# Seven products for both halves of a down-projection's columns, in an encoder trunk on one core

## The chip, the core and the metric

The kernel runs on one core of a Trainium2 chip. The metric is the device time of one execution in microseconds (us). The core's engines are TensorE (PE in the profile; its weight loads are PEld), VectorE (DVE), ScalarE (ACT), GpSimd (POOL) and SyncE (SP, which issues most transfers). Each works through its own instructions in the program's order and meets the others at semaphores.

## The reference

Two layers over 256 positions of 2048 channels, all float32. Each layer is a mixer (pooling and attention in layer 0, a bidirectional mLSTM in layer 1) and then a gated MLP. The change concerns the MLP alone:

```
def conv_ffn(x, w_up, conv_w, conv_b, w_down):     # D_MODEL 2048, D_FF 5632
    u = x @ w_up                                   # 2 * D_FF columns
    up = jnp.pad(u, ((0, 0), (1, 1), (0, 0)))
    u = c[0] * up[:, :-2] + c[1] * up[:, 1:-1] + c[2] * up[:, 2:] + conv_b
    gate, val = jnp.split(u, 2, axis=-1)
    return (jax.nn.silu(gate) * val) @ w_down      # 5632 x 2048

x = x + conv_ffn(rms_norm(x, norm_ffn[layer]), w_up[layer], ..., w_down[layer])
```

## The kernel before

**Arithmetic.** Every float32 operand of a matmul is split into a high part (rounded to TensorE's fp32r) and a low part, the remainder. A product is three matmuls: high by high, high by low, low by high. Weights are split on the fly: ScalarE casts a raw tile to its high part (L120), VectorE subtracts to get the low part (L121).

**The weight stream.** All weights pass through one list of tiles of 128 x 1024 (512 KB), in the order in which TensorE needs them (class Stream, L79 to L142). Raw tiles (w) have six buffers, split tiles (hl) four. Loads go out on SP up to five tiles ahead, splits are placed up to two tiles ahead of the use. Two kinds of entry are special. A `Sum` tile is loaded on SP from one array, and a second array is then added into it by an accumulating transfer that GpSimd issues (L105, L106); Sum tiles have two buffers and are prepared up to ten entries ahead. A `Chain` tile's raw weights get the Sum tile before it added to their first half (L116), and that half is then added to their second half (L117), both on VectorE, before the split.

**One gated MLP** (ffn_layer, L906). The 5632 hidden channels are 44 tiles of 128, in chunks of 4, 8, 8, 8, 8, 8 (FCH, L33). For each hidden tile an *up* (L924) multiplies 2048 channels into gate and value: four weight tiles, 64 matmuls. Its result is gathered (L400, L401), scaled (L928), convolved (L933 to L937), gated (L941, L942) and split into g (L943, L944). The 128 gated channels of 256 positions are two quarters of 128 x 128.

**Down-projection.** The 2048 columns are four blocks of 512. For chunks 0 to 4, blocks 0 and 1 go the ordinary way (down, L1040): for each block the chunk's hidden tiles are accumulated in PSUM and added to x (residual, L407). Blocks 2 and 3 use a 2x2 scheme of seven products instead of eight (Strassen's, in Winograd's form): two hidden tiles by two position tiles on one side, two hidden tiles by two blocks on the other. The sums of g quarters are formed and split by combine (L948); the sums of weight blocks come from Sum and Chain tiles and from a tile prepared on the host. A *unit* A (L968) does four of the products of one pair of hidden tiles (two weight tiles, 12 matmuls), a unit B three (one and a half weight tiles, 9 matmuls). Over a chunk each product accumulates in one PSUM bank; at the end of the chunk's A or B units the banks are added to seven kept sums acc (L991 to L995). After chunk 4 the seven sums are combined into x by eleven additions (total, L999). The last chunk does all four blocks the ordinary way, each in full before the next.

**What sets the order.** _ffn_plan (L1129) writes out the order of ups, units and downs: while chunk c's ups run, the units and the two downs of chunk c - 1 lie between them, one unit per up. The instructions of TensorE stay in this written order. The order on the other engines is set by a scheduler that simulates the kernel while building it. Small tasks (class Weave, L145) are started by estimated time.

Of the kernel before, what the change touches and what calls it, by code (L numbers as in the profile page):

```python
# [31 lines left out]
FT = DFF // P  # L32
FCH = [4, 8, 8, 8, 8, 8]  # L33
CH = 8
NEG = -1.0e30
NGATE = 96 + 8
WARM = 5
# [153 lines left out]
def trunk(ctx: ExitStack, tc: tile.TileContext, gx, xT, xn, call, catt, cml, weights, out):  # L191
# [714 lines left out]
    def ffn_layer(layer, norm, nxt):  # L906
        with ExitStack() as es:
# [7 lines left out]
            combos, pss = {}, {}  # L915

            def cw(tl, j):
                c = C_CONV + layer * 88 * 4 + tl * 4 + j
# [5 lines left out]
            def up(c, f, gt, i):  # L924
                ps = stat_group(xx, list(range(KT)), f"up{layer}_{f}")
                wv.until(lambda: norm.R is not None)
                u = gather(tp, ps, f"up{layer}_{f}")
                v.tensor_mul(u, u, bc(norm.R, 2))  # L928
                y = tp.tile([P, 2, S], F32, tag="y", name=f"y{layer}_{f}")
                z = t1p.tile([P, 2, 2, S], F32, tag="z", name=f"z{layer}_{f}")  # L930
                for j in range(2):
                    tl = f + j * FT
                    a.activation(z[:, 0, j, :], u[:, j, :], AF.Copy, scale=cw(tl, 0))  # L933
                    a.activation(z[:, 1, j, :], u[:, j, :], AF.Copy, scale=cw(tl, 2))
                    a.activation(y[:, j, :], u[:, j, :], AF.Identity, scale=cw(tl, 1), bias=cw(tl, 3))  # L935
# [4 lines left out]
                s_ = pair[-1][:, i % 2 * 2 : i % 2 * 2 + 2].rearrange("p a b -> p (a b)")  # L940
# [3 lines left out]
                v.tensor_sub(gt[:, i, 1, :], s_, gt[:, i, 0, :].bitcast(F32))  # L944
                if i % 2 and c < len(FCH) - 1:
                    combine(c, i // 2, pair[-1])

            def combine(c, j, g4):  # L948

                sf = t1p.tile([P, 4, P], F32, tag="sf", name=f"sf{layer}_{c}_{j}")  # L950
                v.tensor_sub(sf[:, 0:2], g4[:, 0::3], g4[:, 1:2].to_broadcast([P, 2, P]))
# [13 lines left out]
                mm(ps, xl, wh, False, last)  # L965
                wv.tick(0.68)

            def unit(kind, c, j):  # L968

                n = FCH[c] // 2  # L970
                order = (4, 6, 5, 3) if kind == "A" else (0, 1, 2)
                if j == 0:
                    for e in order:
                        pss[e] = psp.tile([P, 512], F32, tag="ps", name=f"pp{layer}_{c}_{e}")
                gt = gts[c]
                s3, s1 = combos[c, j]

                def part(k, t):
                    return [gt[:, 2 * j + k, i, t * P : t * P + P] for i in range(2)]

                if kind == "A":
                    xs = [[s3[:, i, m] for i in range(2)] for m in (1, 0, 2)] + [part(1, 1)]
                else:
                    xs = [part(0, 0), part(1, 0), [s1[:, i] for i in range(2)]]
                for m, e in enumerate(order):
                    if m % 2 == 0:
                        hl = st.next()
                    wh, wl = (hl[:, i, m % 2 * 512 : m % 2 * 512 + 512] for i in range(2))
                    product(pss[e], xs[m], wh, wl, j == 0, j == n - 1)
                if j == n - 1:  # L990
                    for e in order:  # L991
                        if c == 0:
                            a.copy(acc[:, e], pss[e])
                        else:
                            v.tensor_add(acc[:, e], acc[:, e], pss[e])  # L995
                    if kind == "B" and c == len(FCH) - 2:
                        wv.add(total(), 12.0)

            def total():  # L999

                p1, p2, p3, q4, p5, q6, p7 = (acc[:, e] for e in range(7))
                x00, x01, x10, x11 = (x[:, t, c : c + 512] for t in range(2) for c in (1024, 1536))
                steps = [(q6, v.tensor_sub, p1), (x10, v.tensor_sub, q6), (x10, v.tensor_add, p7),
                         (x10, v.tensor_add, q4), (x00, v.tensor_add, p1), (x00, v.tensor_add, p2),
                         (q6, v.tensor_sub, p5), (x01, v.tensor_add, q6), (x01, v.tensor_sub, p3),
                         (x11, v.tensor_add, q6), (x11, v.tensor_sub, p7)]
# [3 lines left out]
                pss["total"] = True  # L1010

            def down_end(gt, b, kts):

# [26 lines left out]
            def down(c, b):  # L1040
                gt, last = gts[c], c == len(FCH) - 1
                kts = list(range(FCH[c]))
                if last and nxt is None and b == NB - 1:
                    down_end(gt, b, kts)
                    return
                ps = mmp.tile([P, 2, 512], F32, tag="mm", name=f"dn{layer}_{c}_{b}")
                mov_part(ps, lambda k: gt[:, k], kts, True, True)
                if last and b >= 2:
                    wv.until(lambda: "total" in pss)
                residual(ps, b)  # L1050
                if last and nxt is None:
                    nc.sync.dma_start(out[:, :, b * 512 : b * 512 + 512], x[:, :, b * 512 : b * 512 + 512])
                elif last:
                    nxt.add(b)

            wv.add(norm.finish(), 4.0)
            f, gts, pair = 0, [], []
            for kind, c, i in _ffn_plan():
                if kind == "up":
                    if i == 0:  # L1060
                        gts.append(actp.tile([P, 8, 2, S], F32R, tag=f"B{c % 2}", name=f"g{layer}_{c}"))
# [1 line left out]
                    f += 1  # L1063
                elif kind == "down":
                    down(c, i)
                else:
                    unit(kind, c, i)

    norms = [Norm(0), None]
    norms[1] = Norm(1)  # L1070
# [55 lines left out]
    return np.ascontiguousarray(t.transpose(4, 0, 2, 1, 3, 5)).reshape(FT * (KT // 4), P, CH * P)  # L1126


def _ffn_plan():  # L1129

    seq = []
    for c, n in enumerate(FCH):
        pairs = FCH[c - 1] // 2 if c else 0
        for i in range(n):
            seq.append(("up", c, i))
            if i < 2 * pairs:
                seq.append(("AB"[i // pairs], c - 1, i % pairs))  # L1140
            for b in range(2):
                if pairs and i == (b + 1) * pairs // 2 - 1:
                    seq.append(("down", c - 1, b))
    return seq + [("down", len(FCH) - 1, b) for b in range(NB)]


def _down_chunks(w):
# [2 lines left out]
    out, k0 = [], 0  # L1150
    for c, n in enumerate(FCH):
        rows = w[k0 * P : (k0 + n) * P]
        out += [_mov(rows[:, b * 512 : b * 512 + 512]) for b in range(2 if c < len(FCH) - 1 else NB)]
        k0 += n
    n = sum(FCH[:-1]) // 2
    b = w[: 2 * n * P, 1024:].reshape(n, 2, P, 2, 512)
    b11, b12, b21, b22 = (b[:, k, :, c] for k in range(2) for c in range(2))

    def two(a, b):
        return np.concatenate([a, b], axis=2)  # L1160

    return np.concatenate(out), two(b12, b12), two(b11, b22), two(b22, b21), two(b11, b21), b22


def _ffn_weights(up, parts):

    down, s0, s1, r, ba, bb = parts
    out, u, d = [], 0, 0
    starts = []
    for c, n in enumerate(FCH):  # L1170
        starts.append(d)
        d += n // 2 * (2 if c < len(FCH) - 1 else NB)
    for kind, c, i in _ffn_plan():
        q = sum(FCH[:c]) // 2 + i
        if kind == "up":
            out += up[u : u + 4]
            u += 4
        elif kind == "down":
            n = FCH[c] // 2
            out += down[starts[c] + i * n : starts[c] + i * n + n]  # L1180
        elif kind == "A":
            out += [Sum(s0[q], s1[q]), Chain(r[q])]
        else:
            out += [ba[q], bb[q]]
    return out


# [98 lines left out]
```

## Time and profile before

| | before |
|---|---|
| median of 3 runs | 2185.68 us (2185.67 to 2186.78) |
| the profiled execution | 2185.79 us |
| its span | 2184.0 us |
| gated MLP of layer 0, first to last up | about 256 to 932 us of the span |
| gated MLP of layer 1, first to last up | about 1458 to 2135 us |
| bytes moved | 462.95 MB, 212 GB/s on the average |

The span is the time from the first to the last instruction that the profiler shows. Busy times are shares of the span; a matmul's end is modelled, so a TensorE that is busy all the time isn't necessarily at its peak. In a row of instructions, "out<-in" names the tiles written and read, "x12" is a count, and a bracket or a last column names what ended the idle time before. "Landing" is the time from a transfer's issue to its completion. A chunk's part of the MLP in which eight ups run with the previous chunk's units and downs is called a full stage below; there are four in a layer (chunks 2 to 5), and the one of chunk 1 carries half as much down work.

### The profile page before, as it was taken

What the parts mean: (1) busy time and instruction counts of PE and PEld (TensorE: products, weight loads), DVE (VectorE), ACT (ScalarE), POOL (GpSimd) and SP (SyncE); (2) the same over time, 40 slices, a digit from 0 to 9 for tenths busy, and PEclk for the clock granted to TensorE, in tenths of its full rate; (3) what the DMA queues carried; (4) which work ended last, traced back from release to release, by engine and by line L of the source; (5) the groups of instructions that cost most, each with busy time, mean ns of one, the idle gap of its engine ahead of it and who ended that gap; (6) DMA issues with size and microseconds to landing.
All of it is one profiled execution on the core that took longest, in us unless ns stands there. A gap on an engine that the chain in (4) does not pass through costs nothing.

```text
span 2184.0 us, 31216 instructions
## 1 busy us (share of the span) xinstructions
PE 2176.3 (100%) x11508; PEld 1862.4 (85%) x11508; DVE 1668.1 (76%) x2358; ACT 1373.8 (63%) x2174; POOL 59.3 (3%) x76
## 2 busy tenths in 40 slices
PE   9999999999999999999999999999999999999999
PEld 7888888888888888889888888888888888888887
DVE  7686687887878788786767676668788787878876
ACT  7665577766667576666555554557776676757663
POOL 0010000000000000000000000000000000000000
PEclk9999999999999999999999999999999999999999
DMA  9556567676777766656565555756768677776664
GB/s 322 182 169 203 175 205 228 210 243 208 249 231 245 223 226 219 217 187 205 161 201 180 181 179 176 224 177 202 229 207 245 207 246 235 246 228 221 219 217 153
DMA packets 133595, 462.95 MB, mean 212 GB/s; under 512 B 14810, under 2 KB 17154, under 8 KB 133442
## 3 DMA queue, kind: packets, MB, share of 16 engines
q1 hardware_dynamic: 125024, 438.08, 60.0%
q0 software_dynamic: 5344, 19.14, 5.2%
q10 hardware_dynamic: 3074, 3.75, 0.7%
q8 instruction: 90, 1.47, 0.3%
q14 instruction: 63, 0.52, 0.1%
HBM read 458.76 MB, written 2.14 MB: 211 GB/s over the span
## 4 chain that ended last, share of the span: by engine, by line
PE 99%; DVE 0%; ACT 0%; issue 0%
PE up L237 45%; PE dn L237 12%; PE op L237 8%; PE pp L237 8%; PE mv L237 4%; PE mq L237 4%; PE mk L237 4%; PE mo L237 4%; PE qproj L237 3%; PE kproj L237 1%; PE pool L237 1%; PE vproj L237 1%; PE qk L237 1%; PE av L237 1%; PE end L237 0%; PE xt L288 0%
## 5 line engine op out<-in xcount | busy, mean ns | idle before, releaser
L121 DVE TENSOR_TENSOR hl<-w,hl 128x1024 fp32r<-128x1024 f32 (+2 forms) x808 | 951.7, 1192 | 256.9 <-ACT hl L120 254.5
L120 ACT CAST hl<-w 128x1024 fp32r<-128x1024 f32 (+2 forms) x807 | 817.1, 1028 | 460.9 <-PE up L237 143.7
L237 PE MATMUL up<-xx,hl 128*128 128x512 f32 (+1 forms) x5632 | 993.6, 337 | 0.0
L237 PEld LDWEIGHTS up<-xx,hl 128*128 128x128 f32 x5632 | 867.0, 188 | 130.4
L237 PE MATMUL dn<-hl,g 128*128 128x512 f32 x1200 | 278.5, 390 | 2.5 <-DVE g L944 2.3
L237 PEld LDWEIGHTS dn<-hl,g 128*128 128x128 f32 x1200 | 224.5, 188 | 50.8 <-DVE g L944 3.2
L400 ACT COPY tb_up<-up 128x512 f32<-128x512 f32 x88 | 51.7, 587 | 135.3 <-PE up L237 135.3
L237 PE MATMUL pp<-hl,s 128*128 128x512 f32 x432 | 111.2, 393 | 0.0
L401 DVE TENSOR_TENSOR tb_up<-up,tb_up 128x512 f32<-128x512 f32 x88 | 60.7, 690 | 57.0 <-ACT tb_up L400 57.0
L935 ACT ACTIVATE y<-tb_up,cst 128x256 f32<-128x256 f32 x176 | 103.8, 590 | 0.0
L936 DVE TENSOR_TENSOR y<-y,z 128x510 f32<-128x510 f32 x88 | 60.6, 688 | 52.9 <-ACT y L935 52.4
L933 ACT ACTIVATE z<-tb_up,cst 128x256 f32<-128x256 f32 x176 | 88.5, 503 | 12.2 <-DVE tb_up L928 12.0
L237 PE MATMUL mk<-xx,hl 128*128 128x512 f32 (+1 forms) x512 | 92.2, 337 | 0.0
L237 PE MATMUL mq<-xx,hl 128*128 128x512 f32 (+1 forms) x512 | 92.1, 337 | 0.0
L237 PE MATMUL mv<-hl,xx 128*128 128x512 f32 (+2 forms) x480 | 91.7, 350 | 0.0
L237 PE MATMUL op<-hl,cat 128*128 128x512 f32 x384 | 91.6, 393 | 0.0
L237 PEld LDWEIGHTS pp<-hl,s 128*128 128x128 f32 x432 | 78.5, 188 | 15.1
L237 PE MATMUL mo<-hl,xx 128*128 128x512 f32 x384 | 90.4, 391 | 0.0
L237 PE MATMUL op<-hl,mcat 128*128 128x512 f32 x384 | 89.5, 392 | 0.0
L237 PEld LDWEIGHTS mq<-xx,hl 128*128 128x128 f32 x512 | 79.2, 188 | 11.6
L237 PEld LDWEIGHTS mk<-xx,hl 128*128 128x128 f32 x512 | 79.0, 188 | 11.4
L237 PEld LDWEIGHTS mv<-hl,xx 128*128 128x128 f32 x480 | 78.3, 189 | 11.2
(229 smaller groups left out, 1985.4 us busy)
## 6 DMA issues: line engine op xcount, KB each, us to landing
w<-in_up SPq DMA_DIRECT2D x352, 512.0 KB, 4.3
w<-in_dn SPq DMA_DIRECT2D x176, 512.0 KB, 4.5
w<-in_m_in SPq DMA_DIRECT2D x124, 512.0 KB, 4.1
w<-in_a_in SPq DMA_DIRECT2D x46, 512.0 KB, 4.4
sum<-in_dn SPq DMA_DIRECT2D x36, 512.0 KB, 4.6
sum<-in_dn POOLq DMA_DIRECT2D x36, 512.0 KB, 7.4
w<-in_a_out SPq DMA_DIRECT2D x32, 512.0 KB, 3.5
w<-in_m_out SPq DMA_DIRECT2D x32, 512.0 KB, 4.0
```

Of the source, the lines that this page charges most:

```text
L120: (self.nc.vector.tensor_copy if i + c == 0 else self.nc.scalar.copy)(hl[:, 0, c : c + n], w[:, c : c + n])
L121: self.nc.vector.tensor_sub(hl[:, 1, c : c + n], w[:, c : c + n], hl[:, 0, c : c + n].bitcast(F32))
L237: pe.matmul(out_, lhsT, rhs, start=start, stop=stop, skip_group_check=True)
L400: a.copy(tb, ps[:, :, 1, :])
L401: v.tensor_add(tb, ps[:, :, 0, :], tb)
L933: a.activation(z[:, 0, j, :], u[:, j, :], AF.Copy, scale=cw(tl, 0))
L935: a.activation(y[:, j, :], u[:, j, :], AF.Identity, scale=cw(tl, 1), bias=cw(tl, 3))
L936: v.tensor_add(y[:, :, 1:S], y[:, :, 1:S], z[:, 0, :, 0 : S - 1])
```

## The change

Blocks 0 and 1 of chunks 0 to 4 now go through the seven products too, so the columns have two halves (h = 0, 1) with units of their own. Where two halves of eight units stand against eight ups, two units follow each up: AA, AA, BB, BB for half 0, then the same for half 1. Sum and Chain tiles double. Instead of seven kept sums there are three per half: the products that enter only one quarter of the result are added to x at once at the end of a chunk's units, the others to the kept sums; total has six additions per half. The combines are placed in the plan ("mix"), each not ahead of the last A unit that reads the same buffers. In the last chunk, blocks 0 and 1 are done together: hidden tiles 0 to 5 for block 0 and for block 1, then tiles 6 and 7 for each.

```diff
+BOTH = (0,1,2,3,4)
...
-            acc = kp.tile([P, 7, 512], F32, tag="acc", name=f"acc{layer}")
+            acc = kp.tile([P, 2, 3, 512], F32, tag="acc", name=f"acc{layer}")
...
-                    pair.append(tp.tile([P, 4, P], F32, tag="silu", name=f"s{layer}_{f}"))
+                    quads[c, i // 2] = tp.tile([P, 4, P], F32, tag="silu", bufs=3, name=f"s{layer}_{f}")
...
-            def unit(kind, c, j):
+            def unit(kind, c, h, j):
...
-                if j == n - 1:
-                    for e in order:
-                        if c == 0:
-                            a.copy(acc[:, e], pss[e])
+                if j < n - 1:
+                    return
+                x00, x01, x10, x11 = parts_of_x(h)
+                if kind == "A":
+                    for to, e in zip(range(3), order):
+                        to = acc[:, h, to]
+                        if h in seen:
+                            v.tensor_add(to, to, pss[e])
                         else:
-                            v.tensor_add(acc[:, e], acc[:, e], pss[e])
-                    if kind == "B" and c == len(FCH) - 2:
-                        wv.add(total(), 12.0)
+                            a.copy(to, pss[e])
+                    seen.add(h)
+                    v.tensor_add(x10, x10, pss[3])
+                else:
+                    v.tensor_add(x00, x00, pss[0])
+                    v.tensor_sub(acc[:, h, 2], acc[:, h, 2], pss[0])
+                    v.tensor_add(x00, x00, pss[1])
+                    v.tensor_sub(x01, x01, pss[2])
+                    if c == len(FCH) - 2:
+                        wv.add(total(h), 12.0 if h else 2.0)
...
+            def down_two(c):
+
+                gt, n = gts[c], FCH[c]
+                pss2 = [mmp.tile([P, 2, 512], F32, tag="mm", name=f"dn{layer}_{c}_{b}") for b in range(2)]
+                for kts in (range(n - 2), range(n - 2, n)):
+                    for ps in pss2:
+                        mov_part(ps, lambda k: gt[:, k], list(kts), kts[0] == 0, kts[-1] == n - 1)
+                wv.until(lambda: 0 not in seen or ("total", 0) in pss)
+                for b, ps in enumerate(pss2):
+                    residual(ps, b)
...
+def _halves(c):
+
+    return () if c == len(FCH) - 1 else (0, 1) if c in BOTH else (1,)
...
         pairs = FCH[c - 1] // 2 if c else 0
+        units = [(kind, c - 1, h, j) for h in (_halves(c - 1) if c else ()) for kind in "AB" for j in range(pairs)]
+        per = max(1, len(units) // n)
+
+        busy = {u[3]: k // per for k, u in enumerate(units) if u[0] == "A"}
         for i in range(n):
             seq.append(("up", c, i))
-            if i < 2 * pairs:
-                seq.append(("AB"[i // pairs], c - 1, i % pairs))
-            for b in range(2):
-                if pairs and i == (b + 1) * pairs // 2 - 1:
-                    seq.append(("down", c - 1, b))
-    return seq + [("down", len(FCH) - 1, b) for b in range(NB)]
+            seq += units[i * per : i * per + per]
+            if len(_halves(c - 1)) == 1:
+                for b in range(2):
+                    if pairs and i == (b + 1) * pairs // 2 - 1:
+                        seq.append(("down", c - 1, b))
+            if c < len(FCH) - 1:
+                seq += [("mix", c, j) for j in range(n // 2) if i == max(2 * j + 1, busy.get(j, 0))]
+    return seq + [("two", len(FCH) - 1, 0)] + [("down", len(FCH) - 1, b) for b in range(2, NB)]
```

More of the change, by code (lines that the diff above doesn't have):

```diff
@@ L1065, in ffn_layer @@
                     down(c, i)
+                elif kind == "two":
+                    down_two(c)
+                elif kind == "mix":
+                    combine(c, i)
                 else:
-                    unit(kind, c, i)
+                    unit(kind, c, i, *j)
     norms = [Norm(0), None]
@@ L1152, in _down_chunks @@
         rows = w[k0 * P : (k0 + n) * P]
-        out += [_mov(rows[:, b * 512 : b * 512 + 512]) for b in range(2 if c < len(FCH) - 1 else NB)]
+        blocks = [_mov(rows[:, b * 512 : b * 512 + 512]) for b in range(NB) if b // 2 not in _halves(c)]
+        if c == len(FCH) - 1:
+            b0, b1 = blocks[:2]
+            blocks[:2] = [b0[:-1], b1[:-1], b0[-1:], b1[-1:]]
+        out += blocks
         k0 += n
     n = sum(FCH[:-1]) // 2
-    b = w[: 2 * n * P, 1024:].reshape(n, 2, P, 2, 512)
-    b11, b12, b21, b22 = (b[:, k, :, c] for k in range(2) for c in range(2))
+    res = [np.concatenate(out)]
     def two(a, b):
         return np.concatenate([a, b], axis=2)
-    return np.concatenate(out), two(b12, b12), two(b11, b22), two(b22, b21), two(b11, b21), b22
-def _ffn_weights(up, parts):
[L1167 to L1174, printed above, removed]
+    for h in range(2):
+        b = w[: 2 * n * P, 1024 * h : 1024 * h + 1024].reshape(n, 2, P, 2, 512)
+        b11, b12, b21, b22 = (b[:, k, :, c] for k in range(2) for c in range(2))
+        res += [two(b12, b12), two(b11, b22), two(b22, b21), two(b11, b21), b22]
+    return res
+def _ffn_weights(up, parts):
+    down = iter(parts[0])
+    out, u = [], 0
+    for kind, c, i, *j in _ffn_plan():
         if kind == "up":
@@ L1177, in _ffn_weights @@
             u += 4
[L1178 to L1184, printed above, removed]
+        elif kind in ("down", "two"):
+            out += [next(down) for _ in range(FCH[c] // 2 * (2 if kind == "two" else 1))]
+        elif kind != "mix":
+            s0, s1, r, ba, bb = parts[1 + 5 * i : 6 + 5 * i]
+            q = sum(FCH[:c]) // 2 + j[0]
+            out += [Sum(s0[q], s1[q]), Chain(r[q])] if kind == "A" else [ba[q], bb[q]]
     return out
@@ L1275, in ffn @@
     def ffn(l):
-        return _ffn_weights(chunks(f"up{l}"), [chunks(f"dn{l}{j}") for j in range(6)])
+        return _ffn_weights(chunks(f"up{l}"), [chunks(f"dn{l}{j}") for j in range(11)])
     n = 3 * (MD + 32)
```

39 lines of the change are left out of this document (21 added, 18 removed).

## The prediction

> **What bounds the kernel now.** I read the page's shares first, then the chain that ended last, then a table of one stage, then the waits, then single instructions.
>
> ```profile
> span 2184.0 us, 31216 instructions
> PE 2176.3 (100%) x11508; PEld 1862.4 (85%) x11508; DVE 1668.1 (76%) x2358; ACT 1373.8 (63%) x2174; POOL 59.3 (3%) x76
> ...
> PE 99%; DVE 0%; ACT 0%; issue 0%
> ```
>
> TensorE is never idle for long, and the chain is 99% TensorE. The profiled execution took 2185.79 us, 1.8 around its span and 0.1 above the median of the runs (2185.68); I count against 2185.8. So fewer matmuls are worth their full time, as long as the other engines go on delivering ahead of TensorE. How near they are shows in one full stage of a gated MLP (eight up tiles with one chunk's down work among them), with this row's columns stretch, length, busy PE, PEld, DVE, ACT, POOL, clock, DMA share, GB/s:
>
> ```profile
> 566.91:697.07 130.16, 130.16 (x693) 111.61 (x693) 106.80 (x143) 87.50 (x136) 3.44 (x4) 1.00 0.74 234
> ```
>
> VectorE is busy 82% of it, ScalarE 67%, the transfers 74%. The clock is full.
>
> **What is removed from TensorE.** From the chain in order of time:
>
> ```profile
> 436.75 2.77 PE pp L237 x12
> 439.52 10.88 PE dn L237 x48
> ...
> 502.29 11.14 PE up L237 x64
> 515.48 11.14 PE up L237 x64
> ```
>
> A block of 512 columns of a chunk of 8 costs 10.88 us in 48 matmuls (0.227 each). Two blocks, shared over four pairs, are 5.44 us per pair. The seven products cost an A unit, 2.77, and a B unit, 13.19 - 11.14 = 2.05 (the distance of the two up rows less one up): 4.82. Each pair saves 0.62. Chunks 0 to 4 have 18 pairs, two layers 36: **-22.3 us**. By count alone, 108 matmuls of 0.227 are 24.5; I take 22.3, since units carry their own overhead. A full stage falls from 130.16 to 127.7.
>
> Blocks by turns put K tiles 6 and 7 after 72 matmuls instead of 36 following the last up, so their last g is ready:
>
> ```profile
> L237 PE MATMUL dn<-hl,g 128*128 128x512 f32 x1200 | 278.5, 390 | 2.5 <-DVE g L944 2.3
> ```
>
> That wait for g is 2.3 us over both layers and goes: **-2.3 us**. Both blocks' additions to x and their transposes then lie beside blocks 2 and 3; no wait follows. TensorE alone would give 2185.8 - 22.3 - 2.3 = 2161.2.
>
> **What is added elsewhere.**
>
> ```profile
> L121 DVE TENSOR_TENSOR hl<-w,hl 128x1024 fp32r<-128x1024 f32 x762 | 920.7, 1221 | 247.4 <-ACT hl L120 245.1
> ...
> L120 ACT CAST hl<-w 128x1024 fp32r<-128x1024 f32 x762 | 787.9, 1051 | 424.3 <-PE up L237 119.8 <-PE dn L237 69.2 <-PE op L237 68.7
> ```
>
> ```profile
> 578.91 0.42 DVE L951 TENSOR_TENSOR sf<-s 128x256 f32<-128x256 f32 x1
> 579.25 0.42 DVE L944 TENSOR_TENSOR g<-s,g 128x256 fp32r<-128x256 f32 x1
> ...
> 645.57 3.49 DVE L121 TENSOR_TENSOR hl<-w,hl 128x1024 fp32r<-128x1024 f32 x3
> ...
> 671.77 1.27 DVE L995 TENSOR_TENSOR acc<-acc,pp 128x512 f32<-128x512 f32 x2
> ```
>
> Back to back, VectorE's instructions overlap a little: three of 1.22 take 3.49, so one costs 1.14 of the queue; one of 512 columns 0.6, one of 256 0.34, one of 128 about 0.2. Per full stage the change adds four whole splits (8 ordinary weight tiles go, 12 come: 4.6), four half ones (2.4), eight chain additions of L116 and L117 (4.8) and five drains (11 become 16: 3.0). VectorE goes from 106.8 to 121.6 of 127.7 us, 95%. ScalarE gets as many casts, about 6 us, to 73%: hidden. Transfers: 8 tiles of 0.52 MB go and 9.4 MB come on 30.5 MB, 35.7 MB or 280 GB/s. On the average it fits. The later combines (beside units), a third silu buffer and the smaller acc wait for nothing new: I price them at 0. So too the order on the issuing queues: a Sum's load waits on SP for its buffer, but the weight loads behind it wait for buffers that come free later still, and GpSimd issues twice as many accumulations with 3.4 of 130 us busy. The additions that put the kept sums into x stand in the last chunk's up part (first half) and beside blocks 0 and 1 (second half).
>
> What doesn't fit is the order. Units now come in twos after an up: four weight tiles lasting 1.39 each (A), or 1.37, 0.69, 1.37, 0.69 (B). Only four split buffers exist, so ScalarE may cast a tile once TensorE has finished the tile four before it. Behind an up that is three tiles of 2.79 ahead; behind two B units it is 0.69 + 1.37 + 0.69 = 2.75 us, and cast and subtraction need 1.05 + 1.22 + waking, 2.4. Nothing may stand in VectorE's queue then. Something does:
>
> ```profile
> DVE w L116 <- DMA w<-in_dn: 37.2, 27, 3.0
> ```
>
> ```profile
> 584.64 0.33 SPq L100 DMA_DIRECT2D w<-in_dn  x1
> ```
>
> ```profile
> 588.95 0.69 DVE L116 TENSOR_TENSOR w<-w,sum 128x512 f32<-128x512 f32 x1 [3.01 <-DMA w<-in_dn]
> 589.56 1.22 DVE L121 TENSOR_TENSOR hl<-w,hl 128x1024 fp32r<-128x1024 f32 x1
> ```
>
> The addition of a Sum tile into its Chain tile (L116) is placed early and waits for a transfer: 27 of 36 times today, 37.2 us in all. Here the load was issued at 584.64, VectorE went on at 588.95 (4.3 us later), and a split behind it, whose cast had been over, came at 589.56. TensorE had three up tiles in hand and noticed nothing. After the change there are 72 such additions, and the built program's order puts the first one of each half between the split of the last B tile and that of the first up tile:
>
> ```
> split 174, tb_up add, split 175, product with R, CHAIN ADD 181, split 176 (up), 2 drains, chain 181, split 177, drain, CHAIN ADD 183, ...
> split 180 (Sum, frees its buffer) ... split 185, CHAIN ADD 189, sf, y add, chain 189, sf, split 186 (up), CHAIN ADD 191, ...
> ```
>
> Tiles 172 to 175 are the B units, 180 to 183 and 188 to 191 the A units. **First ledger**, zero when TensorE ends tile 170. Split 174 ends at 2.4 and frees the raw buffer into which Chain 181 is loaded.
>
> ```profile
> w<-in_dn SPq DMA_DIRECT2D x176, 512.0 KB, 4.5
> ...
> sum<-in_dn SPq DMA_DIRECT2D x36, 512.0 KB, 4.6
> sum<-in_dn POOLq DMA_DIRECT2D x36, 512.0 KB, 7.4
> ```
>
> It lands about 4.45 later, 6.85; chain add to 7.45, split 176 to 8.65. TensorE ends 171 at 2.79 and two B units at 6.9, and needs the low half after two matmuls, 7.35: **1.3 lost**. Without lead, VectorE then has 6.5 us of queue (splits 177 and 178, seven of 0.6) against two up tiles, 5.57: **0.9 more**.
>
> **Second ledger**, zero when split 180 ends. TensorE is then 2.25 us short of tile 180: split 180 ends 9.4 us of queue after split 176, while TensorE has the rest of 176 (2.34), three up tiles (8.36) and the 0.9 ahead of it, 11.6. Sum 188 uses the buffer that 180 frees: load 4.6, accumulation 7.4, wakings 0.35, so 12.35. Chain add and five instructions to split 186 are 3.5: 15.85. TensorE: 2.25 + 4 x 1.39 + 2 x 2.79 + 0.45 = 13.8. **2.05 lost**, and about 0.5 at the next two boundaries, where four short tiles meet a VectorE without slack.
>
> One half therefore costs 4.75 us. Each layer has eight halves with two units per up (two for each of chunks 1 to 4). The first has no pair of B units ahead of it, and in the last the chain add stands one up tile later in the queue; the other six, twelve in two layers, have this form: 57. The four odd ones take 0 to 2.5 each by the same ledger; at 0.8 they are 3. Sum: **+60 us**, and 2185.8 - 22.3 - 2.3 + 60 = **2221 us**.
>
> **Both ends.** No row shows a split behind four short tiles, so the price hangs on landings; it isn't below nothing, because a queue that stands still gives TensorE no time back.
>
> ```profile
> DMA to landing us min/median/max: 3.4/4.6/6.5
> ```
>
> ```profile
> DMA to landing us min/median/max: 5.4/7.4/11.4
> ```
>
> ```profile
> 571.28 0.33 SPq L100 DMA_DIRECT2D w<-in_dn  x1
> ```
>
> ```profile
> 577.17 0.69 DVE L116 TENSOR_TENSOR w<-w,sum 128x512 f32<-128x512 f32 x1 [1.09 <-DMA w<-in_dn]
> ```
>
> These are the load of a Sum, its accumulation, and a Chain load that took 5.9. With the least (3.4, 5.4) the first ledger loses 0.3 + 0.3 and the second nothing: 12 x 0.6 = 7, 2168. With 5.9 for the Chain the first loses 2.75 + 0.9; with 6.5 and 9 for the Sum the second loses 5.5: 12 x 9.2 = 110, 2271. I take the medians: A units today run among such traffic. [...]
>
> **The rivals.** (1) *The cover holds; TensorE's saving is the result: 2161.* It holds if VectorE's chain adds find their data: load 3.1 us or less after the release in the first ledger, load and accumulation 10.3 or less in the second. For it: today's TensorE waits for 27 late adds nowhere, and a VectorE stopped on TensorE has time. Against it: the shortest lead today is longer than 2.75 us. This is the faster side; it decides at 24.6 / 12 = 2.05 us lost per half. [...] Chance 0.21, with stalls up to 20 us in it (2161 to 2181). (2) *Losses equal the saving:* 2.05 per half, 2181 to 2190. 0.06. (3) *The transfers saturate:* an up with two A units moves 5.2 MB in 16.7 us, 314 GB/s, and landings stretch to the heavy end: 2250 to 2280 and over. 0.18. (4) *The forecast,* 2190 to 2250: 0.55.
>
> **How the numbers follow.** Likeliest 2221. The range 2164 to 2268 leaves out about 0.1 on each side. Faster by over 0.2% (4.4 us, about what a measurement can tell here from no change) is rival 1: 0.21; within it 0.06; slower, rivals 3 and 4: 0.73.
>
> **What would show it.** Right: pp rows x1512, dn x336; PE's idle time at up tiles that follow B units, released by the split's subtraction (L121), each 1 to 3 us, and again two up tiles into the second A pair; VectorE's wait at the chain add (L116) far above 37.2 us (72 additions; some 12 x (1.5 + 3.5) + others, 70 to 120); half a stage of about 68 us where a whole one without loss is 127.7. Wrong: PE busy 99% with stages of 127 to 128 us (rival 1), or PE waiting on drains or PSUM instead, or DMA share at 0.95 and more throughout (rival 3).

## The result and the profile after

The changed kernel takes **2272.22 us** (median of 4 runs, 2269.69 to 2275.36), the kernel before 2185.84 beside it (2185.67 to 2186.78): a ratio of 1.0393 [1.0381, 1.0405]. It is slower by 86 us; the forecast was 2221, and its range ended at 2268. The profiled execution took 2269.69 us, 1.8 of it around the span. In the changed kernel every line of the Stream and of the matmul helper stands one line further down (the subtraction of a split is L122, the addition of a Sum into its Chain tile L117, a Sum's load L106 and its accumulation L107).

The page of the changed kernel, span, engines, chain of work that ended last, two groups, and the landings of a Sum tile's load and accumulation:

```profile
span 2267.9 us, 31613 instructions
PE 2189.2 (97%) x11400; PEld 1852.3 (82%) x11400; DVE 1789.4 (79%) x2556; ACT 1426.4 (63%) x2244; POOL 90.1 (4%) x112
...
PE 69%; DVE 13%; DMA 13%; issue 4%; ACT 1%; DVEq 0%; POOLq 0%; ACTq 0%
...
L238 PE MATMUL up<-xx,hl 128*128 128x512 f32 (+1 forms) x5632 | 1029.8, 342 | 70.6 <-DVE hl L122 70.6
...
L117 DVE TENSOR_TENSOR w<-w,sum 128x512 f32<-128x512 f32 x72 | 49.6, 689 | 95.5 <-DMA sum<-in_dn 76.2
...
sum<-in_dn SPq DMA_DIRECT2D x72, 512.0 KB, 4.7
sum<-in_dn POOLq DMA_DIRECT2D x72, 512.0 KB, 8.7
```

TensorE has the 108 matmuls less (11,508 to 11,400), and yet it is idle for 2267.9 - 2189.2 = 78.7 us where it was idle for 7.7, and busy for 12.9 us more than before. The chain that was 99% TensorE is now 69% TensorE, and VectorE and the transfers have 13% each. The third row gives 70.6 of the 78.7 us one place: up tiles, which wait for the split's subtraction on VectorE. The fourth row gives VectorE's: the addition of a Sum tile into its Chain tile, which waits for the Sum's accumulation, 76.2 us of it.

One half stage of layer 0, TensorE's rows in order of time (start, length, instructions, in brackets the idle time ahead and who ended it):

```profile
694.54 0.61 PE L238 MATMUL up<-xx,hl 128*128 128x512 f32 x2
696.77 6.01 PE L238 MATMUL up<-xx,hl 128*128 128x256 f32 x32 [1.61 <-DVE hl L122]
703.23 5.40 PE L238 MATMUL up<-xx,hl 128*128 128x256 f32 x30 [0.45 <-DVE hl L122]
...
713.96 6.19 PE L238 MATMUL up<-xx,hl 128*128 128x512 f32 x34
721.56 5.40 PE L238 MATMUL up<-xx,hl 128*128 128x256 f32 x30 [1.40 <-DVE hl L122]
726.79 2.24 PE L238 MATMUL pp<-hl,s 128*128 128x512 f32 x9
```

And VectorE's rows at the same two places:

```profile
694.89 0.69 DVE L117 TENSOR_TENSOR w<-w,sum 128x512 f32<-128x512 f32 x1 [1.75 <-DMA w<-in_dn]
695.50 1.22 DVE L122 TENSOR_TENSOR hl<-w,hl 128x1024 fp32r<-128x1024 f32 x1
...
718.47 0.69 DVE L117 TENSOR_TENSOR w<-w,sum 128x512 f32<-128x512 f32 x1 [3.39 <-DMA sum<-in_dn]
...
720.28 1.22 DVE L122 TENSOR_TENSOR hl<-w,hl 128x1024 fp32r<-128x1024 f32 x1
```

They are to be read together. After the two B units TensorE does two matmuls of the next up (694.54) and stops; VectorE has been standing for 1.75 us at an addition whose Chain tile is being loaded, and the subtraction that TensorE needs comes behind it (695.50 to 696.72). TensorE goes on at 696.77. That is the first ledger. At 718.47 VectorE has stood for 3.39 us at an addition whose Sum tile is being accumulated, and TensorE's up waits 1.40 us. That is the second.

### The profile page after: what moved, and what is told of

Same layout as the page of the kernel before. It is cut to its first block, busy times and chain, and to the rows that moved or that the text cites. A ratio compares the mean times of both kernels' runs of the same rounds, so it can differ in the third digit from the quotient of the medians.

```text
span 2267.9 us, 31613 instructions
## 1 busy us (share of the span) xinstructions
PE 2189.2 (97%) x11400; PEld 1852.3 (82%) x11400; DVE 1789.4 (79%) x2556; ACT 1426.4 (63%) x2244; POOL 90.1 (4%) x112
## 4 chain that ended last, share of the span: by engine, by line
PE 69%; DVE 13%; DMA 13%; issue 4%; ACT 1%; DVEq 0%; POOLq 0%; ACTq 0%
PE up L238 26%; DMA sum<-in_dn 8%; PE op L238 8%; DVE hl L122 7%; PE pp L238 6%; DMA w<-in_dn 5%; PE mv L238 4%; PE mq L238 4%; PE mk L238 4%; PE mo L238 4%; PE dn L238 3%; PE qproj L238 3%; ACT hl L121 1%; PE pool L238 1%; PE kproj L238 1%
## 5 line engine op out<-in xcount | busy, mean ns | idle before, releaser
L122 DVE TENSOR_TENSOR hl<-w,hl 128x1024 fp32r<-128x1024 f32 (+1 forms) x844 | 978.3, 1170 | 231.2 <-ACT hl L121 228.8
L121 ACT CAST hl<-w 128x1024 fp32r<-128x1024 f32 (+1 forms) x843 | 839.2, 1010 | 436.7 <-PE up L238 118.6
L238 PE MATMUL up<-xx,hl 128*128 128x512 f32 (+1 forms) x5632 | 1029.8, 342 | 70.6 <-DVE hl L122 70.6
L238 PE MATMUL pp<-hl,s 128*128 128x512 f32 x864 | 224.3, 394 | 2.9 <-DVE hl L122 2.7
L238 PEld LDWEIGHTS pp<-hl,s 128*128 128x128 f32 x864 | 159.5, 189 | 37.8 <-DVE hl L122 5.8
L238 PE MATMUL pp<-hl,g 128*128 128x512 f32 x648 | 171.4, 391 | 0.0
L238 PEld LDWEIGHTS pp<-hl,g 128*128 128x128 f32 x648 | 118.7, 188 | 23.5
L121 ACT CAST hl<-sum 128x1024 fp32r<-128x1024 f32 x72 | 75.3, 1046 | 92.1 <-PE up L238 59.8
L117 DVE TENSOR_TENSOR w<-w,sum 128x512 f32<-128x512 f32 x72 | 49.6, 689 | 95.5 <-DMA sum<-in_dn 76.2
L107 POOL DMA_DIRECT2D sum<-in_dn x72 | 61.8, 859 | 1333.6 <-DMA sum<-in_dn 666.2
```

The costliest lines, as they stand in the source:

```text
L107: self.nc.gpsimd.dma_start(w, self.srcs[i].other, accum_op=ALU.add)
L117: self.nc.vector.tensor_add(w[:, :half], w[:, :half], self.sum[:, :half])
L121: (self.nc.vector.tensor_copy if i + c == 0 else self.nc.scalar.copy)(hl[:, 0, c : c + n], w[:, c : c + n])
L122: self.nc.vector.tensor_sub(hl[:, 1, c : c + n], w[:, c : c + n], hl[:, 0, c : c + n].bitcast(F32))
L238: pe.matmul(out_, lhsT, rhs, start=start, stop=stop, skip_group_check=True)
```

## The experiments

The theory under test, A: what costs is VectorE's queue. It runs in order, and an addition that waits for a transfer holds up the splits behind it, which have all that they need. The rivals were B, VectorE has too much to do in a full stage (95% by the forecast's count), and C, the transfers are too many or land too late. In the later expectations C is narrower: a Sum's buffer is released too shortly ahead of the tile's own use, wherever the addition stands; D is then the number of transfers. In the table each ratio is to the kernel before in the same session, whose median was 2185.84 to 2187.60 us.

| kernel | us, median | ratio to before | TensorE busy, idle in the span |
|---|---|---|---|
| the change | 2272.22 | 1.0393 [1.0381, 1.0405] | 2189.2, 78.7 |
| additions directly behind their Sum's split | 2259.08 | 1.0331 [1.0316, 1.0347] | 2193.3, 66.0 |
| additions two tiles ahead | 2236.75 | 1.0230 [1.0215, 1.0245] | 2182.3, 56.0 |
| three Sum buffers (and one of y) | 2238.00 | 1.0236 [1.0218, 1.0254] | 2180.7, 53.8 |
| one buffer of y alone | 2286.73 | 1.0448 [1.0412, 1.0484] | 2194.4, 88.0 |
| two tiles ahead, three Sum buffers | **2171.13** | 0.9927 [0.9912, 0.9942] | 2158.4, 11.0 |
| the same, two silu buffers, y with two | 2171.20 | 0.9927 [0.9914, 0.9941] | 2158.0, 11.5 |
| without accumulations | 2193.73 | 1.0031 [1.0019, 1.0044] | 2165.0, 29.3 |
| without additions | 2163.38 | 0.9894 [0.9880, 0.9909] | 2154.5, 6.9 |
| without both | 2160.47 | 0.9879 [0.9862, 0.9895] | 2153.1, 5.1 |
| additions on GpSimd | 2238.68 | 1.0232 [1.0217, 1.0248] | 2181.0, 55.9 |
| the same, three Sum buffers | 2217.56 | 1.0138 [1.0123, 1.0154] | 2175.3, 41.3 |
| only half 1 by seven products | 2182.61 | 0.9979 [0.9970, 0.9989] | 2175.7, 5.5 |

### What the saving is worth: no additions, no accumulations

```diff
-        self.nc.gpsimd.dma_start(w, self.srcs[i].other, accum_op=ALU.add)
...
-        elif isinstance(self.srcs[i], Chain):
-            half = CH * P // 2
-            self.nc.vector.tensor_add(w[:, :half], w[:, :half], self.sum[:, :half])
-            self.nc.vector.tensor_add(w[:, half:], w[:, half:], w[:, :half])
```

> Neither the chain additions nor the accumulations: the weights are used as loaded, TensorE's instructions stay the same. All theories: 2161, plus or minus 5, the saving that the working gives TensorE alone (108 matmuls and the wait for g). If it stays over 2175, the saving itself was mis-sized or splits of short tiles cost TensorE time without any chain.

2160.47 us, and the forecast's figure for TensorE alone was 2161.2. Every plain load is still made. So the matmuls and the wait for g were priced right together, and all of the rest, 2272.2 - 2160.5 = 111.8 us, is lost on the way. This kernel is the floor below.

### Only the additions left out

```diff
-        elif isinstance(self.srcs[i], Chain):
-            half = CH * P // 2
-            self.nc.vector.tensor_add(w[:, :half], w[:, :half], self.sum[:, :half])
-            self.nc.vector.tensor_add(w[:, half:], w[:, half:], w[:, :half])
```

> The chain additions on VectorE are left out (a Chain tile is used as it was loaded), the loads and accumulations of the Sum tiles stay, so the transfers are those of the changed kernel. Theory A: nothing stands in VectorE's queue in wait for a transfer until the Sum tile itself is cast, some four tiles later: 2161 to 2180, TensorE idle under 25 us. Rival D (the transfers as such make TensorE wait, or the cast of a Sum tile waits as long as the addition did): 2220 or more. In between, say 2195: half and half.

2163.38 us. The Chain tiles are used as loaded; every transfer of the changed kernel is still there. TensorE's waits are then:

```profile
PE up L234 <- DVE hl L118: 1.7, 3, 0.6
PE wps L258 <- DVE pad L626: 1.2, 1, 1.2
```

Theory A's number. The 72 accumulations cost 2163.4 - 2160.5 = 2.9 us by themselves (the loads of Sum and Chain tiles are in both kernels): the rival that transfers as such are too many is out.

### Only the accumulations left out

```diff
-        self.nc.gpsimd.dma_start(w, self.srcs[i].other, accum_op=ALU.add)
```

> The accumulating transfers are left out: a Sum tile is one plain load, so the weight sums lack one addend and GpSimd issues nothing. VectorE's and TensorE's work is the same. Theory A: the loop of load and accumulation shrinks from 13.6 to about 5 us, as in the run with three Sum buffers: 2190 to 2225 us. Theory B: 2240 or more, since VectorE has the same work. Theory C: the DMA share falls from 0.82 to about 0.70 and the time to 2161 to 2185, the wait behind the B units too.

2193.73 us. Each Sum is then one matrix in place of two; all of VectorE's work is still there:

```profile
PE 2165.0 (99%) x11400; PEld 1842.6 (84%) x11400; DVE 1789.7 (82%) x2556; ACT 1426.0 (65%) x2244; POOL 28.2 (1%) x40
```

1789.7 us of VectorE against 1789.4 with the change, and 78 us less time: the amount of VectorE's work isn't the bound, so rival B is out. What is left over the floor, 33 us, goes with additions that wait for loads alone (the scheduler, given a Sum that is there sooner, also places them earlier here, 48 of 72 five tiles ahead):

```profile
DVE w L116 <- DMA w<-in_dn: 14.7, 12, 2.7
```

with 21.6 us of TensorE's waits at up tiles, the first ledger by itself. Taken together: the accumulations without the additions cost 3 us, the additions without the accumulations 33, both 112. It is the meeting of the two in one queue.

### The additions put later, by two distances

```diff
+            self.tc.keep_in_program_order(
+                self.nc.vector.tensor_add(w[:, :half], w[:, :half], self.sum[:, :half]))
-            self.nc.vector.tensor_add(w[:, :half], w[:, :half], self.sum[:, :half])
...
+    st.tc = tc
```

> The addition of the Sum tile into its Chain tile is kept in program order on VectorE: behind the split of its own Sum tile instead of up to seven splits ahead. Nothing else changes. Theory A (additions placed early stop VectorE's queue while their transfers land, and four short weight tiles leave too little lead): most of the loss goes; the Sum's landing then has to come only before its own cast, two up tiles later; 2161 to 2190 us, and VectorE's wait at the addition falls from 95 us to under 20. Theory B (VectorE's work, 95% of a stage, is the bound): the work is the same, so 2240 us or more. Theory C (the transfers saturate): the bytes are the same, so 2240 or more, with the waits moved to the casts.

2259.08: a miss, 13 us in place of some 80 to 110. All 72 additions stand between the split of their Sum tile and that of their Chain tile, which the next expectation calls one tile ahead; the scheduler had 70 of them ahead of the split of a tile three to six before the Chain's own. The waits at the up tiles are nearly gone (3.9 us), but others are there, in the units' tiles (pp):

```profile
PE pp L240 <- ACT hl L122: 29.1, 26, 2.1
PE pp L240 <- DVE hl L123: 27.7, 34, 1.7
```

In order of time, inside an A unit:

```profile
657.78 0.49 PE L240 MATMUL pp<-hl,s 128*128 128x512 f32 x1 [0.94 <-ACT hl L122]
659.12 1.06 PE L240 MATMUL pp<-hl,s 128*128 128x512 f32 x2 [0.85 <-DVE hl L123]
```

In this order the Sum's subtraction, two additions, the cast and the subtraction of the Chain tile follow one another (1.22 + 0.6 + 0.6 + 1.05 + 1.22 = 4.7 us) while TensorE takes 1.39 per tile: the wait has only moved. So the additions were put two tiles ahead, in front of the split of the tile before their Sum:

```diff
+        j = i + 2
+        if j < len(self.srcs) and isinstance(self.srcs[j], Chain):
+            self.chain(j)
...
+    def chain(self, j):
+        half = CH * P // 2
+        w = self.w[j][0]
+        self.tc.keep_in_program_order(
+            self.nc.vector.tensor_add(w[:, :half], w[:, :half], self.w[j - 1][0][:, :half]))
+        self.nc.vector.tensor_add(w[:, half:], w[:, half:], w[:, :half])
```

> The pinned additions of the run before stood behind the split of their own Sum tile, 72 times one tile ahead of their use, and turned the wait of the up tiles into one inside the A units. Here each stands ahead of the split of the tile before its Sum (two tiles ahead), later than the scheduler's three to six and earlier than one. Theory A (the price is where VectorE's queue stands still): the addition no longer stands ahead of the first up tiles' splits behind two B units, nor of split 186, so both ledgers' idle time goes: 2165 to 2200, waits of up tiles on the split's subtraction under 25 us (they were 70.6 and 99.4), waits of A units on casts and subtractions under 15 us (with one tile ahead they were 29.1 and 27.7). Rival C (a half simply has too little time between a Sum buffer's release and its use, wherever the addition stands): within 25 us of 2259, with the waits inside the A units as before.

2236.75: short of theory A's 2165 to 2200, and just inside rival C's 25 us of 2259. TensorE's and VectorE's largest waits of this kind:

```profile
PE pp L243 <- DVE hl L126: 48.5, 38, 4.0
PE up L243 <- DVE hl L126: 1.4, 3, 0.6
```

```profile
DVE w L114 <- DMA sum<-in_dn: 78.3, 30, 4.7
```

The wait for a Chain's load (19.1 us in the changed kernel) is gone from VectorE, and with it the first ledger: up tiles wait 1.4 us in all. The wait for the accumulation is as long as ever (78.3, it was 76.2): two tiles ahead of its use the Sum isn't there yet. Rival C is right about this part.

### A third buffer for Sum tiles

```diff
-        w = self.sums.tile([P, CH * P], F32, tag="sum", name=f"sum{i}")
+        w = self.sums.tile([P, CH * P], F32, tag="sum", bufs=3, name=f"sum{i}")
...
-                y = tp.tile([P, 2, S], F32, tag="y", name=f"y{layer}_{f}")
+                y = tp.tile([P, 2, S], F32, tag="y", bufs=1, name=f"y{layer}_{f}")
```

> A third Sum buffer (room made by one y buffer instead of two), so a Sum no longer waits for the split of the Sum two before it. The early additions stay. Theory A: the wait in the second up with A units (the longer of the two) goes with the clock that it costs, about 3 to 5 us for each of 16 halves; the wait behind two B units for a Chain tile's own load stays, 1.3 to 2 us with its knock-on: 2190 to 2225 us. Theory B or C: within 15 us of 2272.

2238.00, 34 us less, between the two theories' numbers. With the scheduler's order:

```profile
DVE w L117 <- DMA sum<-in_dn: 31.5, 10, 3.8
DVE w L117 <- DMA w<-in_dn: 25.6, 22, 2.6
```

The wait for accumulations falls from 76.2 to 31.5, and the one for Chain loads rises from 19.1 to 25.6: the scheduler, with a Sum that is there sooner, puts the additions earlier still (48 of 72 stand five tiles ahead, where it was 28). The y buffer that made room is a second change in the same run, and has a control of its own:

> Control for the third Sum buffer: only the one buffer of y taken away, as both runs with three Sum buffers had to, with two Sum buffers and the scheduler's order. If y's second buffer matters to nothing: within 4 us of 2272. If the one buffer costs something, it is seen as ScalarE waiting for it, and the third Sum buffer by itself would be worth more than the 34 us measured; if it gains, less.

2286.73 us by the median, 14.5 more than the change, a miss of the 4 us expected. The four runs spread over 16 us (2275.09 to 2290.93), and the lowest is no longer than the change's highest (2275.36), so the size is uncertain. ScalarE's waits for y hardly change (26.7 us, it was 24.0); what rises is VectorE's wait for accumulations, 86.9 us for 76.2. If the two effects simply add, the third Sum buffer alone is worth 34 to 49 us; that wasn't run.

### Both together

> The same order with a third buffer for Sum tiles (and one for y less, for the room), so that a Sum's load and accumulation start one Sum tile sooner. Theory A: both causes are taken away, 2161 to 2185, faster than before, PE busy within 5 us of 2152 (2176.3 less 108 matmuls of 0.227). Rival C (time between release and use): about 30 us under the run with two Sum buffers, as the third buffer gave 34 with the scheduler's order. Rival D (transfers as such are too many): 2230 or more.

**2171.13 us**, ratio 0.9927 [0.9912, 0.9942]: 101 us under the change, and the first complete version of the change that is faster than the kernel before. Theory A's number, with both of its causes gone; TensorE is busy for 2158.4 us, 1.4 more than the 5 us around 2152 allowed. Two stretches of 69 us (stretch, length, busy PE, PEld, DVE, ACT, POOL, clock, DMA share, GB/s; a half stage was that long in the changed kernel and is 64 us here), and TensorE's waits in the units:

```profile
594.00:663.00 69.00, 69.00 (x370) 58.76 (x369) 63.08 (x88) 48.38 (x76) 3.44 (x4) 1.00 0.85 275
663.00:732.00 69.00, 68.83 (x364) 58.52 (x363) 63.65 (x88) 50.34 (x79) 3.44 (x4) 1.00 0.87 281
```

```profile
PE pp L243 <- DVE hl L126: 5.3, 10, 1.3
```

VectorE is busy 91 to 92% of such a stretch, the transfers 85 to 87% at 275 to 281 GB/s, and TensorE hardly waits. A full stage takes 128.4 to 128.6 us, with VectorE busy for 119.6 to 120.2 of them, where the forecast had 127.7 for one without loss. The accumulations land no sooner than in the changed kernel:

```profile
DMA to landing us min/median/max: 5.3/8.5/14.2
```

As run, neither edit alone is worth more than 36 us, and both are worth 101. Each takes one of two waits from the same queue, and while the other is left VectorE still comes late. Over the floor 10.7 us are left; the kernel without the additions has 2.9. To see whether the single y buffer is in that:

```diff
-                y = tp.tile([P, 2, S], F32, tag="y", bufs=1, name=f"y{layer}_{f}")
+                y = tp.tile([P, 2, S], F32, tag="y", name=f"y{layer}_{f}")
...
-                    quads[c, i // 2] = tp.tile([P, 4, P], F32, tag="silu", bufs=3, name=f"s{layer}_{f}")
+                    quads[c, i // 2] = tp.tile([P, 4, P], F32, tag="silu", bufs=2, name=f"s{layer}_{f}")
```

> The version at 2171 (additions two tiles ahead, three Sum buffers) with the room taken from the third silu buffer in place of the second y buffer, since y with one buffer cost 14 us in the changed kernel (2286.7 to 2272.2). If y's single buffer still costs something there: 2163 to 2170, nearer to the 2163.4 without additions. If with both waits gone nothing hangs on y any more: 2171 plus or minus 1.5. If two silu buffers make ScalarE wait for a late combine: over 2175.

2171.20 (5 runs, 2170.92 to 2171.28): unless two effects cancel, nothing hangs on y or on the third silu buffer any more. The remaining 7.8 us over the kernel without additions are, by the two profiles, 4.1 us of TensorE's idle time (11.0 and 6.9) and 3.9 of its busy time; no run takes them apart further.

### The additions on GpSimd

```diff
-            self.nc.vector.tensor_add(w[:, :half], w[:, :half], self.sum[:, :half])
-            self.nc.vector.tensor_add(w[:, half:], w[:, half:], w[:, :half])
+            self.nc.gpsimd.tensor_add(w[:, :half], w[:, :half], self.sum[:, :half])
+            self.nc.gpsimd.tensor_add(w[:, half:], w[:, half:], w[:, :half])
```

> The two chain additions of each Chain tile are issued on GpSimd (90 of 2268 us busy) in place of VectorE, two Sum buffers as in the changed kernel. Theory A (what costs is VectorE's queue standing at an addition whose data are under way): VectorE's queue never stands, TensorE's waits at up tiles after B units vanish, 2165 to 2200. Against it: on GpSimd the additions stand ahead of the next pair's accumulations, and an addition that waits for a Chain's load holds them up; the length of a GpSimd addition of 128x512 is not known from any row here (on VectorE 0.69 us; if it is over 3 us, four of them per A pair of units and the accumulations behind them come too late). Rival (time between release and use, wherever the addition stands): 2235 to 2275, with TensorE waiting in the A units.

> Additions on GpSimd and three Sum buffers. Theory A: 2161 to 2180, at or under the 2171 of three buffers with VectorE's additions put in place by hand, because 72 x 2 additions leave VectorE's queue (about 79 us of its 1787). If a GpSimd addition is longer than some 3 us, or if it slows VectorE while both run: over 2200.

2238.68 with two Sum buffers and 2217.56 with three: both misses for A's numbers. The first lies in the rival's 2235 to 2275, and TensorE's waits are mostly where that rival (C above) had them, in the units (pp):

```profile
PE pp L238 <- DVE hl L122: 28.7, 37, 1.3
PE up L238 <- DVE hl L122: 18.1, 35, 1.0
```

So with two Sum buffers too little time between a buffer's release and its use is part of the price here too, as with the additions two tiles ahead; with three, the units' wait falls to 5.8 us. VectorE's queue no longer stands at an addition, and 34 us are gained, but something else is paid, as the second expectation allowed for (over 2200). GpSimd's groups with three buffers, and VectorE's subtractions there and in the changed kernel:

```profile
L117 POOL TENSOR_TENSOR w<-w,sum 128x512 f32<-128x512 f32 x72 | 152.3, 2116 | 665.0 <-DMA w<-in_dn 491.1 <-DVE x L1003 59.5 <-DVE hl L122 47.7
L118 POOL TENSOR_TENSOR w<-w 128x512 f32<-128x512 f32 x72 | 137.7, 1913 | 5.8
```

```profile
L122 DVE TENSOR_TENSOR hl<-w,hl 128x1024 fp32r<-128x1024 f32 x762 | 976.5, 1299 | 216.8 <-ACT hl L121 214.6
```

```profile
L122 DVE TENSOR_TENSOR hl<-w,hl 128x1024 fp32r<-128x1024 f32 x762 | 921.4, 1220 | 228.5 <-ACT hl L121 226.2
```

An addition takes 1.9 to 2.1 us on GpSimd where it is 0.69 on VectorE, and VectorE's subtraction rises from 1220 to 1299 ns, 55 us over the 762. Within one stretch:

```profile
682.61 1.83 POOL L117 TENSOR_TENSOR w<-w,sum 128x512 f32<-128x512 f32 x1
684.51 2.15 POOL L118 TENSOR_TENSOR w<-w 128x512 f32<-128x512 f32 x1
```

```profile
683.20 4.54 DVE L122 TENSOR_TENSOR hl<-w,hl 128x1024 fp32r<-128x1024 f32 x2
```

Two subtractions that take 2.36 us elsewhere take 4.54 beside GpSimd's additions. No run shows by what the one slows the other.

### Half of the change alone

```diff
-BOTH = (0,1,2,3,4)
+BOTH = ()
```

> Only one half of the columns by seven products, as before, with three kept sums, the later combines and the last chunk's first two blocks by turns. By my sum the blocks by turns are worth 2.3 us and the rest nothing: 2182 to 2185 us. If the kept sums or the combines cost something of their own, it is above 2190.

2182.61 us (10 runs), beside 2187.36 for the kernel before: as expected. Blocks by turns, three kept sums and the moved combines are no part of the loss. They gain 4.8 us by the medians (2.4 to 6.6 by the ratio's interval), where 2.3 was forecast.

## Why the prediction went wrong

**The direction, the mechanism and its places held.** The saving on TensorE was right (2161.2 forecast, 2160.47 measured; against the kernel before in the same session, 2187.60, it is 27.1 us where 24.6 was forecast). VectorE's load and the transfers do fit: 95% and 280 GB/s were forecast for a stage, and the kernel at 2171.13 runs its full stages at 93% and 278 to 279 GB/s; the chain additions do stand in VectorE's queue, and VectorE's wait there is 95.3 us for transfers (76.2 + 19.1) where 70 to 120 was given. The faster rival, the cover, would have had no waits. The measured time lies in the third rival's 2250 to 2280, but its mechanism, saturation, is refuted: the kernel without additions has every transfer, and the one at 2171.13 has accumulations that land as late (8.5 us).

**The ledgers, in one half.** The first gave 1.3 and 0.9 us, and the quoted half has 1.61 and 0.45. The second gave 2.05 and about 0.5; there it is 1.40, in the half ahead of it 3.03. The half stage was to take about 68 us: from the second A pair at 658.06 to the next at 726.79 it is 68.7.

**The step that failed is the sum over the halves, "4.75 per half x 12 halves = 57 + 4 odd halves x 0.8 = 3".** 60 us were forecast; against the floor it is 111.8. One of its terms is mis-sized, and one is missing.

- *The four odd halves lose nearly like the others.* The forecast took the first half of each layer to have no pair of B units ahead of it, and the last to have its addition one up later, and put each at 0.8. The first half of layer 0 has idle times of 1.29 and 3.77 us. All of TensorE's waits of 0.25 us and more that end with a split's subtraction are 72.4 us: 56.0 in the twelve regular halves, where 57 was forecast, and 16.4 in the four odd ones, where it was 3. So the 4.75 per half was right as a sum (4.67), though of its parts the first ledger was smaller (1.7 for 2.2) and the second with the boundaries larger (3.0 for 2.55). The accumulation, which lands in 8.7 us where the ledger had 7.4, may be part of the latter.
- *A wait also makes TensorE's busy time longer, and no term of the sum had that.* The two profiled spans are 109.7 us apart (2267.9 and 2158.2 at the floor), and 36.1 of that is TensorE's busy time (2189.2 and 2153.1). Both kernels have the same 11,400 matmuls in the same order, so they can be set side by side one by one. 19.0 of the 36.1 us are in the 141 matmuls that touch a stretch of half clock, 15.2 in the first matmuls behind 56 other waits. Four stretches of the changed kernel, the columns as above, the clock third from the end:

```profile
643.00:648.00 5.00, 5.00 (x30) 4.22 (x28) 0.55 (x2) 2.63 (x4) 0.01 (x1) 1.00 1.04 297
648.00:651.20 3.20, 0.24 (x2) 0.00 (x0) 3.20 (x6) 1.86 (x3) 0.00 (x0) 1.00 0.86 239
651.20:655.00 3.80, 3.73 (x12) 3.15 (x13) 3.55 (x6) 1.09 (x3) 0.00 (x0) 0.56 0.51 169
655.00:659.00 4.00, 4.00 (x24) 3.46 (x23) 4.00 (x7) 1.79 (x3) 0.00 (x0) 1.00 0.86 259
```

The wait ends at 651.27, and for the next 3.8 us the granted clock is 0.56: 12 matmuls where the following 4 us have 24. The rows of the same 30 matmuls of an up show it too:

```profile
651.27 6.95 PE L238 MATMUL up<-xx,hl 128*128 128x256 f32 x30 [3.03 <-DVE hl L122]
```

6.95 us behind this wait, 5.40 behind the waits of 0.45 and 1.40 quoted above. Over the span the mean granted clock is 0.991, against 1.000 in the kernels at 2160 to 2171; 0.009 x 2267.9 is 20 us, which fits the 19.0. The first matmul behind a wait costs something at full clock too:

```profile
696.77 0.39 PE L238 MATMUL up<-xx,hl 128*128 128x256 f32 x1 [1.61 <-DVE hl L122]
```

It adds 0.387 us to the busy time. At the floor, where by the profile the matmul ahead of it is still running when it starts, the same one adds 0.114. That is 0.27 us for each of the 56. It accounts for most of the rest. In the kernel with the additions on GpSimd, whose clock is 0.998, it makes up 20.6 of the 28 us by which TensorE's busy time exceeds the floor's.

With the 72.4 us of waits alone the time would have been 2161.2 + 72.4 = 2233.6, inside the range; what the waits do to the matmuls behind them, 36.1 us, carried it out at the top. The range had been worked out from landings, and its upper end from longer landings; it had no end for what a stall does to the work behind it.

## What to carry to other kernels

An operation that waits for a transfer, in a queue that runs in order, is charged to everything behind it: place it by hand just ahead of its use (here ahead of the split two tiles before: with two Sum buffers directly ahead was too late, three to six tiles too early), and give its data a buffer more: either alone left 76 to 78 us over the floor, both together 11. Price a stall of TensorE as its idle time, the longer first matmul behind it (0.27 us here) and the slow stretch that may follow (19.0 us over eleven here), and count the places where it occurs on the trace of a like stage, not by the exceptions that look exempt. A kernel with the suspected work left out gives the floor in one run, and two more, each with one part left out, tell whether it is the work, the transfers or their meeting in one queue.

## What the hardware showed that wasn't expected

**The granted clock fell behind 11 of the 12 waits of 1.88 to 4.17 us.** Around the first second-A pair of layer 0 in the changed kernel (columns as above):

```profile
438.00:441.20 3.20, 0.00 (x0) 0.00 (x0) 2.48 (x4) 1.02 (x1) 0.00 (x0) 0.81 0.43 172
441.20:446.00 4.80, 4.80 (x15) 4.18 (x16) 4.80 (x7) 1.50 (x4) 0.00 (x0) 0.50 0.62 207
446.00:452.00 6.00, 6.00 (x26) 4.89 (x25) 5.55 (x8) 5.30 (x8) 1.06 (x2) 0.93 0.88 243
```

Of the 32 waits of TensorE of 0.8 us and more that the timeline of the MLPs of this kernel lists, all 20 up to 1.61 us are followed by 4 us at clock 1.00, all 8 of 2.97 us and more (to 4.17) by 0.50 to 0.62, and of the four between, three (1.88, 2.24, 2.76) by 0.63 to 0.69 and one (2.48) by 1.00. The 4 us are an average over two clocks. The trace's own record of the granted clock has only 1.00 and 0.50, in steps of 3.41 us that all lie on one grid (0.50 from 1798.50 to 1801.91, say, behind the wait of 1.88 us that ended at 1797.48). In this kernel the falls go with the idle time within one such step: up to the last matmul there are eleven from 1.00 to 0.50, each behind a step with 1.88 us of idle time or more, and none follows a step with 1.53 or less. The wait of 2.48 us was cut by a step's end into 1.53 and 0.95, and was spared. In the kernel with the additions directly behind their Sum's split the two waits of 0.94 and 0.85 us quoted above lie in one step, 1.79 us together, and are followed by 0.57 over 4 us.

**GpSimd's additions weren't free to VectorE**, as the rows of its experiment show: 79 ns on each subtraction of VectorE's, for 290 us of additions on GpSimd.
